# A streaming encoder layer on one core: loads, w_out's first quarters, gate rows and the last scaling in another order

## The chip, the cores and the metric

The kernel runs on one core of a Trainium2 chip. Its time is the device time of one execution in microseconds (us); lower is better. The core has a matrix engine (TensorE, PE in the profile; the loading of its weights is shown apart as PEld), VectorE (DVE), ScalarE (ACT), GpSimd (POOL) and SyncE (SP). Each engine works through its own instructions in order. Transfers (DMAs) are issued from the queues of SP, ACT and POOL and run on 16 DMA engines.

## The reference

One layer of an encoder, for a prompt of 2048 frames and a sample of 32 frames, all in float32, with a width of 1024:

```python
def layer(h, p, ...):
    hn = rmsnorm(h, g_mix)
    proj = hn @ w_in                       # 1024 -> 3072
    hA, bA, cA, zA, vB, zB = jnp.split(proj, ...)
    yA = bA * causal_conv3(cA * hA) * silu(zA)
    yB = (pooled_means(vB) - vB) @ pool_w * pool_scale * silu(zB)
    h = h + concat([yA, yB]) @ w_out       # 1024 -> 1024
    gate = sigmoid(rmsnorm(h, g_ple) @ w_ple_gate)
    h = h + (p @ w_ple) * gate
    return h, new_conv, new_pool
```

A last `rmsnorm(h, g_final)` gives the outputs; the states of the convolution and of the pooling are outputs too.

## The kernel before

**Precision.** Every float32 operand of a product is split into a rounded part (hi) and a remainder (lo): ScalarE casts hi, VectorE computes lo = source - hi (`split`, L79 to L83). A product is the sum of hi x hi, hi x lo and lo x hi, three matmuls for each 128 rows of the inner dimension.

**Stages.** First the input projection w_in, by blocks of 416 frames; then w_out over pairs of tiles of 128 frames (the products o0, o2, ... o14, and a short last one); then the gate with the final scaling (g0 to g14). The stages of w_out and of the gate use a scheme with seven products for a pair of tiles in place of eight (`seven`, L218): of four quarters of the weights (11, 12, 21, 22) and of four parts of the frames it builds sums (S1 to S4 of the frames, T1 to T4 of the weights). Each product takes twelve matmuls; results collect in the banks x_o, y_o and z_o, and VectorE (`carry`, `out`, L1335 to L1352) takes them out. A product that needs a bank afresh waits for that.

**Who sets the order.** A scheduler orders the instructions of each engine from the program text, its estimates and the dependencies; calls of `keep_in_program_order` fix some of them, and `issue_after` holds back a load until an instruction named there has been issued. A reader of a new tile in a pool waits until the pool's previous tile there is free.

**The beginning** (L627 to L789). The frames of the first block are loaded in four tiles (xt; the fourth, of 64 rows, with two loads). ScalarE squares each tile with a sum (L93), POOL forms 1/root (`rstd_of`, L69 to L77), VectorE scales the frames by root and by g_mix, which lies in two PSUM banks, a half each (`first_normal`, L639), PE transposes, ScalarE casts the hi parts (`first_hi`, L661), VectorE the lo parts (L665). Then come three first products zb, v and c (`first_products`, L619). Their weights are loaded by `raw_weight` (L524) where each is needed in the text: zb at L689, v and c at L707. g_mix is copied from PSUM to SBUF as g_bc by two ScalarE copies (L722). Small rows (conv_w, conv_b, pool_scale, the two caches, g_ple) are loaded at L768 to L775 and turned on PE (pv). The second block's frames xt(1,0..2) are loaded in `second_block` (L726).

**w_out's first pair** (L1403 to L1449). w_out's rows come in as wo_q, two halves of columns each; `layout` (L1403) casts quarters 11, 21 and 22 from them. wo_c holds 21's hi, one wo_d its lo, two others 22's hi and lo. In o0 they are cast as soon as `more` (the parts 12, S4 and 22 of the frames) has been issued: 21 and 22 take turns, row by row. PE needs 21 first, in the product y_o.

**The gate's rows** (`scale_gate`, L1379). w_gate's rows are scaled by g_ple once: in each of eight rounds (k) POOL issues two loads (gs, 256 KB each, ring of two), ScalarE scales them (L1391) and stores them to g_d from its own queue (L1392). A new round's loads wait for the stores of the round before. `next_gate` scales the waiting round and issues the next, at the end of each pair and once within o2. After o0, `done_h` (L1361) squares the two finished tiles on ScalarE; POOL's `rs_h` is the root.

**The end** (`last_pair`, L1563; `normed`, L1609). The last pair's second tile is scaled by its root in two parts: 640 columns on VectorE, stored from SP's queue (L1613, L1614), 384 on ScalarE, stored from ScalarE's.

Of the kernel before, what the change touches and what calls it, by code (L numbers as in the profile page):

```python
# [15 lines left out]
P = 128  # L16
# [18 lines left out]
def trunk(ctx, tc, x_p, x_s, c_conv, c_pool, p_p, p_s, g_mix, w_in, conv_w, conv_b, pool_w,  # L35
# [32 lines left out]

    def rstd_of(ssq, n, name, r=None):  # L69

        ms = sm.tile([P, 1], F32, tag="ms", name=f"ms_{name}")
        nc.gpsimd.tensor_scalar(ms[:n], ssq[:n], scalar1=1.0 / D, scalar2=EPS,  # L72
                                op0=ALU.mult, op1=ALU.add)
        if r is None:
            r = sm.tile([P, 1], F32, tag="rstd", name=f"rstd_{name}")
        nc.gpsimd.tensor_tensor(r[:n], ms[:n], nhalf[:n], op=ALU.pow)  # L76
        return r  # L77
# [110 lines left out]
    def frame_parts(cmb, tmp, name, a11, a12, a21, a22):  # L188

        A = {}

        def put(q, src):
            A[q] = cmb.tile([P, KH, 2, P], F32R, tag="c", name=f"{name}_{q}")
            return split(A[q][:, :, 0], A[q][:, :, 1], src)

        def comb(q, x, y, op):
            t = tmp.tile([P, KH, P], F32, tag="s", name=f"{name}_f{q}")  # L200
            nc.vector.tensor_tensor(t, x, y, op=op)
            return t

        s1 = comb("S1", a21, a22, ALU.add)
        put("11", a11)
        s2 = comb("S2", s1, a11, ALU.subtract)
        put("S2", s2)
        put("S1", s1)
        put("S3", comb("S3", a11, a21, ALU.subtract))

        def more():
            put("12", a12)
            put("S4", comb("S4", a12, s2, ALU.subtract))
            return put("22", a22)

        return A, more
# [125 lines left out]
    with ExitStack() as s1:  # L342
# [61 lines left out]

        def x_load(name, rows):

            t, at = ring4(xin, f"xt_{name}"), 0
            for src in rows:
                m = src.shape[0]
                nc.sync.dma_start(t[at:at + m], src)  # L410
                at += m
            return t, at, f"x{name}"
# [6 lines left out]
        def x_tile(name, rows):  # L419
            return x_stat(x_load(name, rows))  # L420
# [103 lines left out]
        def raw_weight(kind, j, name, ring=raw_ring):  # L524
            t = ring(f"raw_{name}")
            col = cols[kind] * WA + j * P
            raw_loads.append(nc.sync.dma_start(t, w_in[:, col:col + P].rearrange("(k p) n -> p k n", p=P)))
            return t
# [99 lines left out]
        ahead0 = [x_load(f"0_{c}", [x_rows(0, c)]) for c in range(3)]  # L628
        short0 = x_load("0_3", [x_rows(0, 3), x_rows(1, 3)])
        B0.update(six(0))  # L630
# [42 lines left out]

        for c in range(3):
            first_x.append(x_stat(ahead0[c], True))
# [13 lines left out]
        raw = raw_weight("zb", 0, "firstzb")  # L689
# [16 lines left out]
        def other_first(kind):  # L706
            raw = raw_weight(kind, 0, f"first{kind}")  # L707
# [11 lines left out]

        first_w.extend(other_first(kind) for kind in ("v", "c"))  # L720
# [5 lines left out]
        def second_block():  # L726
# [3 lines left out]
            for c in range(3):  # L730
                x = x_tile(f"1_{c}", [x_rows(1, c)])
                normal(x)
                xs.append((x, slice(0, P)))
                yield
# [32 lines left out]

        rows = ftile("rows").rearrange("p k n -> p (k n)")[:112, :P]  # L768
        nc.gpsimd.memset(rows, 0.0)
        nc.sync.dma_start(rows[0:12], conv_w[0].rearrange("r (j c) -> (r j) c", c=P))  # L770
        nc.sync.dma_start(rows[12:16], conv_b[0].rearrange("(j c) -> j c", c=P))
        nc.sync.dma_start(rows[16:20], pool_scale[0].rearrange("(j c) -> j c", c=P))
        nc.sync.dma_start(rows[32:40], c_conv[0, 0].rearrange("r (j c) -> (r j) c", c=P))
        nc.sync.dma_start(rows[40:100], c_pool[0, 0].rearrange("r (j c) -> (r j) c", c=P))
        nc.sync.dma_start(rows[100:108].rearrange("k (q c) -> k q c", q=4), g_ple[0].rearrange("(q k c) -> k q c", q=4, k=KC))  # L775
# [540 lines left out]
    with ExitStack() as s2:  # L1316
        pool = lambda name, bufs: s2.enter_context(tc.tile_pool(name=name, bufs=bufs, reuse_waits="tile"))
        w3, qa, xh, st, ss, cmb = (pool(*a) for a in (
            ("w3", 1), ("qa", 2), ("xh", 3), ("st", 4), ("ss", 3), ("cmb", 8)))

        def quarters(name, W):
            c = halves(slot(f"{name}_c"))
            d = {h: w3.tile([P, KH, NH], F32R, tag=f"d{h}", name=f"{name}_d{h}") for h in (1, 0, 2)}
            W.update({"11": c[:2], "21": (c[2], d[0]), "22": (d[1], d[2])})
# [54 lines left out]
        def scale_gate(k):  # L1379
# [6 lines left out]
            for half, t in enumerate(ts):  # L1386
                nc.gpsimd.dma_start(t, rows[:, :, half * NH:half * NH + NH])
# [26 lines left out]
        def rest():  # L1414

            with tc.issue_after(more().ins):
                layout(["21", "22"])
# [12 lines left out]
        for i in range(0, NT - 1, 2):  # L1430
            with tc.issue_after(loaded[-1].ins):
                x = [load_rows(xh, "x", i + b, x_p) for b in range(2)] if i else [first_x, second_x]
            seven(f"o{i}", S.pop(i), W, *h_ops(x, P, f"o{i}", i == 0), {0: {1: rest}, 2: {3: next_gate}}.get(i, {}), True, i == 0)
# [6 lines left out]
            if i + 2 < NT - 1:  # L1440
# [3 lines left out]
                more()  # L1444
# [118 lines left out]
        def last_pair(i, A, before):  # L1563
# [45 lines left out]
            def normed(b, rf):  # L1609
# [3 lines left out]
                fixed(nc.vector.tensor_scalar(o[:, :cut], o[:, :cut], scalar1=rf, scalar2=None, op0=ALU.mult))  # L1613
                nc.sync.dma_start(y[:, :cut], o[:, :cut])  # L1614
# [159 lines left out]
```

## Time and profile before

| | us |
|---|---|
| median of three runs | 921.37 (920.61 to 921.42) |
| the profiled execution | 921.02 |
| span of the profiled execution | 919.2 |
| busy: PE / DVE / ACT / POOL | 905.7 / 722.4 / 481.2 / 159.8 |

The span runs from the first to the last instruction recorded; 1.82 us of the profiled execution lie around it. A line of the timeline reads: start, duration (both us), engine, line of the program, operation, output <- inputs, shape, how many instructions, and in brackets the idle time before and what ended it. "SPq", "ACTq" and "POOLq" are the instructions that issue DMAs. A line of the chain of waits reads: start, duration, what the end of the run was waiting for then. The rows of DMA issues end with the size of one transfer and the median time from issue to landing.

### The profile page before, as it was taken

The page shows a single profiled execution, that of the slowest core. Times are in us where ns is not written, and L with a number is a line of the kernel's source. Part 1 is how long each engine was busy: PE and PEld are TensorE (multiplying, and loading weights), DVE is VectorE, ACT ScalarE, POOL GpSimd, SP SyncE. Part 2 cuts the span into 40 slices and gives each one's busy share as a digit, 9 for nine tenths or more (in the row PEclk, how much of TensorE's full clock was granted, in tenths as well). Part 3 has the DMA queues.
Part 4 walks back from the last instruction along what each step waited for, and adds up shares of the span by engine and source line. Part 5 has one row for each costly group of instructions (what it writes and reads, how often), then busy time and mean ns, then how long its engine had stood idle before and what let it go on. Part 6 is the DMA issues. An engine that isn't in the chain of part 4 may idle for free.

```text
span 919.2 us, 13202 instructions
## 1 busy us (share of the span) xinstructions
PE 905.7 (99%) x4529; PEld 822.7 (90%) x4529; DVE 722.4 (79%) x1236; ACT 481.2 (52%) x894; POOL 159.8 (17%) x307
## 2 busy tenths in 40 slices
PE   8999999999999999999999999999999999999996
PEld 6999999999999999999999987888878878888885
DVE  6996989999576989795777679665558658889885
ACT  7744565654445555443545356334336755555554
POOL 3111222121000333210000120111203301111113
PEclk9999999999999999999999999999999999999998
DMA  9357687798945898638975469865777984676564
GB/s 262 93 145 217 168 249 230 234 294 287 413 131 168 251 227 225 216 122 296 274 228 173 155 243 291 267 189 177 237 228 231 354 263 143 203 242 235 188 209 169
DMA packets 138447, 205.12 MB, mean 223 GB/s; under 512 B 13116, under 2 KB 101724, under 8 KB 137101
## 3 DMA queue, kind: packets, MB, share of 16 engines
q1 hardware_dynamic: 117773, 139.41, 48.9%
q0 software_dynamic: 17872, 59.45, 19.8%
q10 hardware_dynamic: 2736, 5.44, 1.8%
q8 instruction: 35, 0.57, 0.3%
q14 instruction: 31, 0.25, 0.1%
HBM read 136.60 MB, written 67.64 MB: 222 GB/s over the span
## 4 chain that ended last, share of the span: by engine, by line
PE 91%; DVE 3%; DMA 2%; ACT 2%; issue 1%; POOL 0%; SPq 0%; POOLq 0%; DVEq 0%; ACTq 0%
PE x_g L175 9%; PE x_o L175 9%; PE x_zab L591 7%; PE x_zbv L591 6%; PE x_ch L591 5%; PE z_g L175 5%; PE e L107 4%; PE z_o L175 4%; PE z_zab L591 3%; PE h L591 3%; PE z_zbv L591 3%; PE z_ch L591 3%; PE b L591 3%; PE za L591 3%; PE zb L591 2%; PE c L591 2%
## 5 line engine op out<-in xcount | busy, mean ns | idle before, releaser
L80 ACT CAST y_S<-y_fS 128x512 fp32r<-128x512 f32 x32 | 19.5, 622 | 42.2 <-PE x_o L175 20.4
L175 PE MATMUL x_g<-wg_b,g_S 128*128 128x512 f32 x128 | 35.7, 389 | 0.0
L175 PE MATMUL x_o<-wo_b,y_S 128*128 128x512 f32 x128 | 35.6, 390 | 0.0
L591 PE MATMUL x_zab<-B,w_zab_S 128*128 128x416 f32 x168 | 34.2, 352 | 0.2 <-ACT V L987 0.2
L591 PE MATMUL z_zab<-B,w_zab_S 128*128 128x416 f32 x168 | 34.3, 351 | 0.0
L591 PE MATMUL x_zbv<-B,w_zbv_S 128*128 128x416 f32 x168 | 34.2, 352 | 0.0
L591 PE MATMUL z_ch<-B,w_ch_S 128*128 128x416 f32 x168 | 34.1, 351 | 0.0
L591 PE MATMUL z_zbv<-B,w_zbv_S 128*128 128x416 f32 x168 | 34.0, 351 | 0.0
L591 PE MATMUL x_ch<-B,w_ch_S 128*128 128x416 f32 x168 | 34.0, 351 | 0.0
L107 PE MATMUL e<-wq,pps 128*128 128x512 f32 x144 | 33.1, 390 | 0.0
L591 PEld LDWEIGHTS x_zab<-B,w_zab_S 128*128 128x128 f32 x168 | 31.3, 188 | 0.9 <-ACT V L987 0.5
L107 PEld LDWEIGHTS e<-wq,pps 128*128 128x128 f32 x144 | 27.0, 188 | 5.6
L591 PEld LDWEIGHTS z_zbv<-B,w_zbv_S 128*128 128x128 f32 x168 | 31.4, 188 | 0.3
L591 PEld LDWEIGHTS x_ch<-B,w_ch_S 128*128 128x128 f32 x168 | 31.4, 188 | 0.3
L591 PEld LDWEIGHTS z_ch<-B,w_ch_S 128*128 128x128 f32 x168 | 31.3, 188 | 0.3
L591 PEld LDWEIGHTS z_zab<-B,w_zab_S 128*128 128x128 f32 x168 | 31.3, 188 | 0.3
L591 PEld LDWEIGHTS x_zbv<-B,w_zbv_S 128*128 128x128 f32 x168 | 31.3, 188 | 0.4
L1542 DVE SCALAR_TENSOR_TENSOR h<-h,rstd_f,g_bc 128x1024 f32<-128x1024 f32 (+1 forms) x15 | 19.3, 1284 | 14.0 <-POOL rstd_f L76 14.0
L80 ACT CAST y<-y 128x512 fp32r<-128x512 f32 x24 | 14.8, 618 | 29.4 <-PE z_o L175 12.8
L1335 DVE TENSOR_TENSOR c_o<-x_o,x 128x512 f32<-128x512 f32 x14 | 9.7, 691 | 25.7 <-PE x_o L175 25.7
L72 POOL TENSOR_SCALAR ms_f<-ssq_f 128x1 f32<-128x1 f32 (+1 forms) x15 | 6.6, 441 | 128.8 <-ACT junk L93 128.5
L175 PEld LDWEIGHTS x_o<-wo_b,y_S 128*128 128x128 f32 x128 | 23.9, 188 | 5.2 <-ACT c_o L1340 0.3
(591 smaller groups left out, 2694.9 us busy)
## 6 DMA issues: line engine op xcount, KB each, us to landing
y<-y_d SPq DMA_DIRECT2D x16, 512.0 KB, 6.0
x<-in_x_prompt_dram SPq DMA_DIRECT2D x16, 512.0 KB, 6.0
h_d<-x SPq DMA_DIRECT2D x16, 512.0 KB, 4.3
h<-h_d SPq DMA_DIRECT2D x16, 512.0 KB, 3.5
xt<-in_x_prompt_dram SPq DMA_DIRECT2D x15, 512.0 KB, 7.8
e<-e_d SPq DMA_DIRECT2D x15, 512.0 KB, 5.2
out_dram<-h POOLq DMA_DIRECT2D x14, 512.0 KB, 3.0
p_dT<-T POOLq DMA_DIRECT2D x12, 512.0 KB, 6.0
```

The costliest lines, as they stand in the source:

```text
L72: nc.gpsimd.tensor_scalar(ms[:n], ssq[:n], scalar1=1.0 / D, scalar2=EPS, op0=ALU.mult, op1=ALU.add)
L80: ins = nc.scalar.copy(hi, src)
L107: nc.tensor.matmul(ps, pps[:, a, k], wp[k][b][:, cs], start=k + q == 0, stop=k == 1 and q == 2)
L175: nc.tensor.matmul(ps[:n], lhs[:, k, a, :n], w[b][:, k], start=start and k + q == 0, stop=k == KH - 1 and q == 2, skip_group_check=True)
L591: nc.tensor.matmul(ps[:, :NB], lhs[:, k, x], b[:, k, y], start=start and k + q == 0, stop=stop and k == KH - 1 and q == 2, skip_group_chec ...
L1335: add = lambda o, a, b: nc.vector.tensor_tensor(o, a, b, op=ALU.add)
L1542: nc.vector.scalar_tensor_tensor(h[:n], h[:n], rf[:n], g_bc[:n], op0=ALU.mult, op1=ALU.mult)
```

## The change

1. *Small rows and weights at the start.* The six loads of small rows, without g_ple's, move up to just behind the frames. The weights of zb, v and c are loaded together behind them, and zb's load waits for the landing of the third frame tile. The first tile of the second block is issued behind c's load, then g_ple's rows, then the two other tiles.
2. *w_out's first quarters.* `more` is in three parts. 21 is cast after the part 12 has been issued (step 1 of `seven`), 22 after S4 (step 4), and the part 22 of the frames comes last. One of the lo tiles of 22 moves to a pool of its own (w2).
3. *The gate's rows.* Each root is remembered (`roots`), and scale_gate's loads are issued behind the last one. In POOL's queue the first round's loads so stand behind the two roots of o0's tiles; before, they stood ahead of them.
4. *The last scaling.* The second tile's 640 columns are scaled by VectorE and stored by SP in two pieces of 320.

The changed kernel's line numbers are some 20 higher around the gate (L1391 is L1410 there).

```diff
@@ first lines
+    roots = []
...
-        nc.gpsimd.tensor_tensor(r[:n], ms[:n], nhalf[:n], op=ALU.pow)
+        roots.append(nc.gpsimd.tensor_tensor(r[:n], ms[:n], nhalf[:n], op=ALU.pow))
...
-        def more():
-            put("12", a12)
-            put("S4", comb("S4", a12, s2, ALU.subtract))
+        def more(i):
+            if i == 0:
+                return put("12", a12)
+            if i == 1:
+                return put("S4", comb("S4", a12, s2, ALU.subtract))
             return put("22", a22)
...
-        def raw_weight(kind, j, name, ring=raw_ring):
+        def raw_weight(kind, j, name, ring=raw_ring, behind=None):
...
+            if behind is not None:
+                tc.add_manual_dep(raw_loads[-1].ins, behind.ins.name, mybir.DependencyInfo(
+                    mybir.DependencyClass.Sync, mybir.DependencyReason.DATA), reason="leaves the bandwidth to frames")
...
         ahead0 = [x_load(f"0_{c}", [x_rows(0, c)]) for c in range(3)]
+        third_landed = frame_loads[-1]
         short0 = x_load("0_3", [x_rows(0, 3), x_rows(1, 3)])
+
+        rows = ftile("rows").rearrange("p k n -> p (k n)")[:112, :P]
+        nc.gpsimd.memset(rows, 0.0)
+        nc.sync.dma_start(rows[0:12], conv_w[0].rearrange("r (j c) -> (r j) c", c=P))
...
+        nc.sync.dma_start(rows[40:100], c_pool[0, 0].rearrange("r (j c) -> (r j) c", c=P))
...
+        first_raws = {kind: raw_weight(kind, 0, f"first{kind}", behind=third_landed if kind == "zb" else None)
+                      for kind in ("zb", "v", "c")}
+        with tc.issue_after(raw_loads[-1].ins):
+            ahead1 = [x_load("1_0", [x_rows(1, 0)])]
+        nc.sync.dma_start(rows[100:108].rearrange("k (q c) -> k q c", q=4), g_ple[0].rearrange("(q k c) -> k q c", q=4, k=KC))
...
-        raw = raw_weight("zb", 0, "firstzb")
+        raw = first_raws["zb"]
...
-            raw = raw_weight(kind, 0, f"first{kind}")
+            raw = first_raws[kind]
...
+        ahead1 += [x_load(f"1_{c}", [x_rows(1, c)]) for c in range(1, 3)]
         first_w.extend(other_first(kind) for kind in ("v", "c"))
...
-                x = x_tile(f"1_{c}", [x_rows(1, c)])
+                x = x_stat(ahead1[c])
...
-        w3, qa, xh, st, ss, cmb = (pool(*a) for a in (
-            ("w3", 1), ("qa", 2), ("xh", 3), ("st", 4), ("ss", 3), ("cmb", 8)))
+        w3, qa, w2, xh, st, ss, cmb = (pool(*a) for a in (
+            ("w3", 1), ("qa", 2), ("w2", 1), ("xh", 3), ("st", 4), ("ss", 3), ("cmb", 8)))
...
-            d = {h: w3.tile([P, KH, NH], F32R, tag=f"d{h}", name=f"{name}_d{h}") for h in (1, 0, 2)}
+            d = {h: (w2 if h == 2 else w3).tile([P, KH, NH], F32R, tag=f"d{h}", name=f"{name}_d{h}") for h in (1, 0, 2)}
...
-            for half, t in enumerate(ts):
-                nc.gpsimd.dma_start(t, rows[:, :, half * NH:half * NH + NH])
+
+            with tc.issue_after(roots[-1].ins):
+                for half, t in enumerate(ts):
+                    nc.gpsimd.dma_start(t, rows[:, :, half * NH:half * NH + NH])
...
-        def rest():
-
-            with tc.issue_after(more().ins):
-                layout(["21", "22"])
+
+        def lower_left():
+            with tc.issue_after(more(0).ins):
+                layout(["21"])
+
+        def lower_right():
+            with tc.issue_after(more(1).ins):
+                layout(["22"])
+            more(2)
...
-            seven(f"o{i}", S.pop(i), W, *h_ops(x, P, f"o{i}", i == 0), {0: {1: rest}, 2: {3: next_gate}}.get(i, {}), True, i == 0)
+            seven(f"o{i}", S.pop(i), W, *h_ops(x, P, f"o{i}", i == 0), {0: {1: lower_left, 4: lower_right}, 2: {3: next_gate}}.get(i, {}), True, i == 0)
...
-                more()
+                for part in range(3):
+                    more(part)
...
-                fixed(nc.vector.tensor_scalar(o[:, :cut], o[:, :cut], scalar1=rf, scalar2=None, op0=ALU.mult))
-                nc.sync.dma_start(y[:, :cut], o[:, :cut])
+                for cs in (slice(0, cut // 2), slice(cut // 2, cut)) if b else (slice(0, cut),):
+                    fixed(nc.vector.tensor_scalar(o[:, cs], o[:, cs], scalar1=rf, scalar2=None, op0=ALU.mult))
+                    nc.sync.dma_start(y[:, cs], o[:, cs])
```

The scheduler answers with further moves. At the start, ScalarE's order is: the hi parts of the third tile, the two g_bc copies, the two zb casts, the fourth tile's hi parts, then the casts of v and c; before, the two copies came after v's and c's casts. In o2 (the pair that follows o0), the first round's scalings stand on ScalarE ahead of the cast of S1 of the pair o4; before, they stood ahead of it too, with two casts of y between and after them.

## The prediction: does the time move?

> **What bounds the kernel now.** The page first: its span and its busy shares.
>
> ```profile
> span 919.2 us, 13202 instructions
> PE 905.7 (99%) x4529; PEld 822.7 (90%) x4529; DVE 722.4 (79%) x1236; ACT 481.2 (52%) x894; POOL 159.8 (17%) x307
> ```
>
> TensorE is busy for 905.7 of 919.2 us. No matmul is added or removed, so only the remaining 13.5 us, or a new hole in PE, can change the time. The diff touches three such places: the start, the first pair of h tiles (o0), the end. The start comes next, with the chain of waits and the timeline of each engine:
>
> ```profile
> 1.99 6.16 DMA xt<-in_x_prompt_dram
> ...
> 12.01 1.40 DVE xt L639 x2
> 13.40 0.60 DVE B L661
> 14.01 0.61 DVE B L665
> 14.75 1.37 PE zb L619 x6
> ```
>
> ```profile
> 1.13 2.30 SPq L410 DMA_DIRECT2D xt<-in_x_prompt_dram  x5
> 3.48 0.46 SPq L527 DMA_DIRECT2D raw_firstzb<-in_w_in_dram  x1
> 7.10 2.80 DVE L639 SCALAR_TENSOR_TENSOR xt<-xt,rstd_x,gm 128x512 f32<-128x512 f32 x4 [4.92 <-POOL rstd_x L76]
> 10.50 2.90 DVE L639 SCALAR_TENSOR_TENSOR xt<-xt,rstd_x,gm 128x512 f32<-128x512 f32 x4
> 12.88 1.15 ACT L692 CAST w_firstzb<-raw_firstzb 128x512 fp32r<-128x512 f32 x2
> 13.96 0.43 ACT L661 CAST B<-pt 128x128 fp32r<-128x128 f32 x2
> 16.36 1.08 ACT L722 COPY g_bc<-gm 128x512 f32<-128x512 f32 x2
> ```
>
> The chain names the DMA of the third frame until 8.15. VectorE, though, has no gap from 7.10 to 14.62 except about 0.1 us before 12.01 (four steps from 7.10 to 9.90, one remainder, four from 10.50 to 13.40, a cast, a remainder). It starts at 7.10 on the first frame's root. The first product, at 14.75, ends that run, not the wait for the third frame.
>
> In the middle, ScalarE and TensorE in o0:
>
> ```profile
> 554.20 0.62 ACT L1408 CAST wo_c<-wo_q 128x512 fp32r<-128x512 f32 x1
> 554.72 0.62 ACT L1408 CAST wo_d<-wo_q 128x512 fp32r<-128x512 f32 x1
> ```
>
> ```profile
> 553.46 3.01 PE L175 MATMUL x_o<-wo_b,y_S 128*128 128x512 f32 x12
> ...
> 557.99 1.42 PE L170 MATMUL y_o<-wo_c,y 128*128 128x512 f32 x5 [0.53 <-ACT wo_c L1408]
> ...
> 560.18 2.89 PE L170 MATMUL z_o<-wo_d,y_S 128*128 128x512 f32 x12
> 562.90 2.88 PE L175 MATMUL x_o<-wo_T,y 128*128 128x512 f32 x12
> ```
>
> A product of twelve matmuls takes 2.72 us from start to start (560.18 to 562.90). From 553.46 two of them should bring z_o at 558.90; it comes at 560.18. The casts of w_out's quarters hold PE for 1.28 us.
>
> **The change part by part.**
>
> *Frames and rows.* All five frame loads were issued (by 3.43) before the zb weights' load (3.48), so moving the weights later can at most give the frames bandwidth. Even a third frame landing a microsecond earlier moves only the 0.1 us gap: gain 0 to 0.1, and I take 0. [...]
>
> *ScalarE's order at the start.* In the changed program's order the two g_bc copies stand ahead of the zb casts and of the casts of the fourth frame's block (L661, 128x128), of which the first product needs one. The second copy waits there for the last L639, which reads the same bank and ends at 13.40. From there: copy 0.54 (two take 1.08), two zb casts at 0.54 (12.88 to 13.96), one block cast 0.22 (two take 0.43), issue 0.13 (14.62, the end of 14.01's, to 14.75): 13.40 + 0.02 + 0.54 + 1.08 + 0.22 + 0.13 = 15.39, against 14.75: **+0.64**. The zb load, now issued behind the third frame's landing (8.15), has 5.7 us until its cast at 13.9; 512 KB of w_out took 5.5 (row below). Bounds: -0.1 (the copies hidden, the gap gained) to +1.0 (one more cast step from the later products, whose casts are behind the same two copies, or zb some tenths late). I take **+0.6**; afterwards PE has next to no idle that could absorb it.
>
> *w_out in another order.* ScalarE now does the four wo_c casts (quarter 21) right after y_12, where it stands idle before 552.30, and the wo_d casts of 22 later. The timeline, and the loads' issues:
>
> ```profile
> 552.30 0.62 ACT L80 CAST y_S<-y_fS 128x512 fp32r<-128x512 f32 x1 [3.02 <-PE x_o L175]
> ```
>
> ```profile
> wo_q<-in_w_out_dram SPq DMA_DIRECT2D x4, 512.0 KB, 5.5
> ```
>
> The hole of 3.02 us takes four casts of 0.52 (554.20 to 554.72; 2.1 us); their loads took 5.5 us. Hence the 1.28 us goes: **-1.3** (bounds -1.3 to -0.5, where 22's casts and remainders, now the last in that queue, hold z_o).
>
> *Gate's rows.* The rows of w_gate (L1387, two of 256 KB) are scaled by ScalarE and stored. Their loads stood on POOL ahead of the roots of tiles 0 and 1; now they follow them.
>
> ```profile
> 548.08 1.43 POOL L1387 DMA_DIRECT2D gs<-in_w_ple_gate_dram  x2 [0.91 <-DMA e_d<-eout]
> 568.45 0.55 POOL L76 TENSOR_TENSOR rs_h<-ms_h,nhalf 128x1 f32<-128x1 f32 x1
> 574.91 0.75 POOL L1387 DMA_DIRECT2D gs<-in_w_ple_gate_dram  x1 [5.91 <-ACT y_S L80]
> 579.45 0.69 POOL L1387 DMA_DIRECT2D gs<-in_w_ple_gate_dram  x1 [3.79 <-DMA g_d<-gs]
> ```
>
> ```profile
> 570.20 0.33 ACTq L1392 DMA_DIRECT2D g_d<-gs  x1
> 583.29 1.04 ACT L93 ACTIVATE junk<-x 128x1024 bf16<-128x1024 f32 x1
> 584.79 0.73 ACT L1391 ACTIVATE gs<-gs,vec 128x512 f32<-128x512 f32 x1 [0.36 <-DMA gs<-in_w_ple_gate_dram]
> ```
>
> The loads of stretches of the trace, with their median from issue to landing; the first row is 545 to 575, the second 575 to 600:
>
> ```profile
> gs<-in_w_ple_gate_dram POOLq DMA_DIRECT2D x3, 256.0 KB, 11.1
> gs<-in_w_ple_gate_dram POOLq DMA_DIRECT2D x4, 256.0 KB, 6.7
> ```
>
> With o0 shorter by 1.28 the second root ends at 567.7; the two loads issue at 567.75 and 568.5, not at 548.08 and 548.8. ScalarE waits for them in its queue: behind gs_1 stand y_S of S1 and S3 of the next pair; VectorE has their remainders and two sums before `x<-x_o,c_o`, which empties the bank that PE's x_o of T4 needs:
>
> ```profile
> 573.78 2.88 PE L175 MATMUL x_o<-wo_b,y_S 128*128 128x512 f32 x12
> 576.99 0.69 DVE L1335 TENSOR_TENSOR x<-x_o,c_o 128x512 f32<-128x512 f32 x1
> 581.94 2.88 PE L175 MATMUL x_o<-wo_T,y 128*128 128x512 f32 x12
> 591.66 0.69 DVE L1335 TENSOR_TENSOR c_o<-x_o,x 128x512 f32<-128x512 f32 x1 [2.19 <-PE x_o L175]
> ```
>
> If loads land after 8.5 us (between 11.1 and 6.7, by their place in time), gs_1 starts at 577.0; + 0.65 gs_1, 0.6 cast, four VectorE steps at 0.6 (0.69 in the sum's row, overlapped by 0.1) and the sum itself end at 581.3. PE wants it at 581.94 - 1.28 = 580.66: **0.65 us** of stall. Below 7.8 us there is none; at 11.1 it is 3.3.
>
> The stores of the scaled rows follow at 576.9 and 577.7; the second pair of loads stands behind them, 4.7 us after (570.20's store to 574.91): 581.6 and 582.35, instead of 574.91 and 579.45. The load of 579.45 landed after 5.3 (584.79). With that price they land at 586.9 and 587.7. ScalarE then does twice a scaling (0.65) and a square (1.15 with its read), then two casts (0.55): until 591.6; VectorE's second remainder ends at 592.2, c_o at 592.85. PE's x_o with wo_b comes 7 x 2.72 after 573.78, at 592.82, now 592.82 - 1.28 + 0.65 = 592.2: **0.65 us** more, none if both pairs land 0.65 sooner in sum, 2.4 at 7. By the third k it recovers, since one round of store and load needs 4.7 + 6.7 us of the pair's 7 x 2.72. Together **+1.3**, bounds 0 and +5.
>
> [...]
>
> *Last scaling in pieces.*
>
> ```profile
> 914.39 0.55 DVE L1613 TENSOR_SCALAR hg<-hg,rstd_l 128x640 f32<-128x640 f32 x1 [0.83 <-POOL rstd_l L1606]
> 915.03 0.38 ACTq L1616 DMA_DIRECT2D out_dram<-hg  x1
> ```
>
> A piece of 320 columns takes some 0.35, so the first store leaves at 914.8, the second at about 915.1 to 915.4. ScalarE's own store is issued until 915.41 either way, and the bytes are the same: -0.25 to +0.15, taken as **0**.
>
> Sum: +0.6 - 1.3 + 1.3 + 0 = +0.6. The profiled execution took 921.02 (its span and 1.82 around it), 0.35 below the median of 921.37; +0.6 on the median gives **922.0 us**.
>
> **The rivals.**
>
> 1. *Rows come in time.* POOL's loads share nothing with SP's backlog, or 512 KB less in the stretch before 578 lets the first pair land within 7 us and the second within 5.3. For: the median of 6.7 after 575. Against: the 11.1 of the pair issued in o0. The sum is +0.6 - 1.3 = -0.7, **920.7**. If the start costs nothing too (-1.3): **920.1**, and with a gain at start and end (-0.1 - 0.25) 919.7. [...]
> 2. *Rows come late* (slower). ScalarE, queued behind its gate scalings, keeps PE waiting 2.1 us where the first loads need 10 us, and 2.4 more where the second need 7. It decides from about 9.5 us of the first. +0.6 - 1.3 + 2.1 + 2.4 = +3.8: **925.2**. For: the row of 11.1, and the new issue lies in its stretch; against: that stretch ends at 575, while these loads run.
> 3. *w_out's order doesn't help*, because 22's remainders or the y load hold PE at z_o instead (0.5 of 1.28 gained): 922.0 + 0.8 = **922.8**.
>
> **How the numbers follow.** Forecast 0.40, rows in time 0.25 (a third of it with no loss at the start), rows late 0.23, w_out's order without help 0.12. About 0.2% (1.84 us) is what a measurement of this kernel can tell from no change: 919.5 to 923.2. Faster then holds only in part of rival 1: 0.12. Slower is rival 2 (0.23) and the upper parts of forecast and rival 3, which lie 1.2 and 0.4 below the bound: 0.17; in all 0.40. Same: 0.48. The range of 8 in 10 reaches from rival 1's lower form to between forecast and rival 2's point: **919.8 to 924.8**.
>
> **What would show it.** First product at 15.3 to 15.5 behind ScalarE's block cast (a start at 14.7 refutes the +0.6). No wait of y_o for wo_c; z_o 5.4 us behind x_o's wo_b. POOL's gate loads right behind the second root, ScalarE idle for DMA gs before L1410, and PE idle twice, before x_o of T4 and x_o with wo_b of the next pair, 0.65 each. The prediction is wrong if gs is never waited for, if PE gets idle at any other place, or if the end moves by over 0.3.

## The result: slower, and the profile after

| | before | after |
|---|---|---|
| median | 921.45 us (920.61 to 923.69, 6 runs) | 928.93 us (927.40 to 929.90, 6 runs) |
| ratio to before | | 1.0075 [1.0065, 1.0086] |
| profiled execution / its span | 921.02 / 919.2 us | 928.77 / 926.9 us |

The ratio and its interval are worked out from all the runs, so they need not be the quotient of the two medians. The time lies above the whole range (919.8 to 924.8). First the page of the changed kernel, its span and busy shares, then its waits of PE ("waited for": us in total, times, the longest).

```profile
span 926.9 us, 13209 instructions
PE 908.4 (98%) x4529; PEld 824.4 (89%) x4529; DVE 720.8 (78%) x1237; ACT 480.3 (52%) x894; POOL 160.0 (17%) x307
```

```profile
PE x_o L177 <- ACT y L82: 3.6, 1, 3.6
...
PE zb L628 <- ACT B L679: 1.4, 1, 1.4
```

PE's busy time grew by 2.7 us with the same 4529 matmuls, and its holes by 5. So there are two kinds of loss: waits, and matmuls that ran longer. The second kind shows in the granted clock of the start (0.67 of full speed in 16 to 20 us, 1.00 before). Each row of this view is a stretch, and PEclk stands behind the busy times of the five engines; first the changed kernel, then the kernel before:

```profile
16.00:20.00 4.00, 3.85 (x14) 3.75 (x15) 4.00 (x10) 3.87 (x9) 0.49 (x1) 0.67 1.02 393
20.00:24.00 4.00, 4.00 (x22) 3.90 (x21) 3.01 (x6) 2.77 (x6) 3.58 (x6) 0.90 1.02 283
```

```profile
16.00:20.00 4.00, 4.00 (x23) 3.93 (x22) 3.88 (x9) 3.12 (x7) 0.06 (x1) 1.00 0.95 335
```

In 16 to 20 us PE issued 14 matmuls where it issued 23 before. The trace's clock records put it down to one piece: half clock from 17.39 for 3.41 us. The timeline of the start, changed kernel:

```profile
9.21 0.40 SPq L533 DMA_DIRECT2D raw_firstzb<-in_w_in_dram  x1
9.28 1.06 ACT L95 ACTIVATE junk<-xt 128x1024 bf16<-128x1024 f32 x1 [1.87 <-DMA xt<-in_x_prompt_dram]
13.75 1.15 ACT L748 COPY g_bc<-gm 128x512 f32<-128x512 f32 x2
14.79 1.14 ACT L717 CAST w_firstzb<-raw_firstzb 128x512 fp32r<-128x512 f32 x2
15.83 0.44 ACT L679 CAST B<-pt 128x128 fp32r<-128x128 f32 x2
16.15 2.12 PE L628 MATMUL zb<-B,w_firstzb 128*128 128x416 f32 x8 [1.36 <-ACT B L679]
```

The order on ScalarE is the predicted one (copies, zb casts, block cast, first product). But the third frame was squared at 9.28, and the first product came at 16.15, 1.40 later than before. PE had idled for 1.36 us ahead of it, where it idled for 0.83 before:

```profile
14.75 1.75 PE L619 MATMUL zb<-B,w_firstzb 128*128 128x416 f32 x8 [0.83 <-DVE B L665]
```

In the middle, POOL's loads, ScalarE and PE of the changed kernel:

```profile
571.81 0.90 POOL L78 TENSOR_TENSOR rs_h<-ms_h,nhalf 128x1 f32<-128x1 f32 x1
572.67 1.51 POOL L1406 DMA_DIRECT2D gs<-in_w_ple_gate_dram  x2
582.33 0.72 ACT L1410 ACTIVATE gs<-gs,vec 128x512 f32<-128x512 f32 x1 [9.18 <-DMA gs<-in_w_ple_gate_dram]
584.22 0.72 ACT L1410 ACTIVATE gs<-gs,vec 128x512 f32<-128x512 f32 x1 [1.18 <-DMA gs<-in_w_ple_gate_dram]
589.24 3.01 PE L177 MATMUL x_o<-wo_T,y 128*128 128x512 f32 x12 [3.64 <-ACT y L82]
591.85 0.72 ACT L1410 ACTIVATE gs<-gs,vec 128x512 f32<-128x512 f32 x1 [2.73 <-DMA gs<-in_w_ple_gate_dram]
```

The two loads landed 9.7 and 10.8 us after their issue (572.67 to 582.33; 573.4, the middle of the two, to 584.22). ScalarE stood 9.18 and 1.18 us for them, PE 3.64. And w_out's first pair:

```profile
557.95 2.88 PE L177 MATMUL x_o<-wo_b,y_S 128*128 128x512 f32 x12
560.67 1.98 PE L172 MATMUL y_o<-wo_c,y 128*128 128x512 f32 x8
562.48 1.07 PE L172 MATMUL y_o<-wo_d,y 128*128 128x512 f32 x4
563.39 2.88 PE L172 MATMUL z_o<-wo_d,y_S 128*128 128x512 f32 x12
```

z_o follows wo_b's product by 5.44 us, where it took 6.72: the 1.28 were won (1.14 where every matmul is matched with its own start before).

**Where the time went**, by matching each matmul with the same one before and taking the difference of their starts; the places are times of the kernel before: +2.97 us at 43 us, +3.84 at 152, +4.56 at 471, +4.35 at 556, +3.21 at 560 (w_out's gain), +3.50 at 580, +7.40 at 583 (the gate's rows), +7.63 at 601, +7.9 at the last, and +7.7 for the span.

### The profile page after: what moved, and what is told of

It reads as the page before. It is cut to its first block, busy times and chain, and to the rows that moved or that the text cites. A ratio compares the mean times of both kernels' runs of the same rounds, so it can differ in the third digit from the quotient of the medians.

```text
span 926.9 us, 13209 instructions
## 1 busy us (share of the span) xinstructions
PE 908.4 (98%) x4529; PEld 824.4 (89%) x4529; DVE 720.8 (78%) x1237; ACT 480.3 (52%) x894; POOL 160.0 (17%) x307
## 3 DMA queue, kind: packets, MB, share of 16 engines
q10 hardware_dynamic: 2736, 5.44, 1.8%
## 4 chain that ended last, share of the span: by engine, by line
PE 86%; DMA 5%; DVE 5%; ACT 3%; issue 1%; POOL 0%; SPq 0%; POOLq 0%; DVEq 0%; ACTq 0%
PE x_g L177 9%; PE x_o L177 8%; PE x_zab L600 7%; PE x_zbv L600 6%; PE x_ch L600 5%; PE z_g L177 5%; PE e L109 4%; PE z_o L177 4%; PE z_zab L600 3%; PE z_zbv L600 3%; PE z_ch L600 3%; PE za L600 3%; PE b L600 3%; PE h L600 2%; PE y_g L177 2%; PE zb L600 2%
## 5 line engine op out<-in xcount | busy, mean ns | idle before, releaser
L177 PEld LDWEIGHTS x_g<-wg_b,g_S 128*128 128x128 f32 x128 | 24.0, 188 | 5.0
```

Of the source, the lines that this page charges most:

```text
L177: nc.tensor.matmul(ps[:n], lhs[:, k, a, :n], w[b][:, k], start=start and k + q == 0, stop=k == KH - 1 and q == 2, skip_group_check=True)
```

## The experiments

Each kernel is the kernel before or the changed one with parts exchanged. The kernel before ran beside them each time: median 922.1 for the first four, 921.6 for the next three, 922.0 for the last five.

| | kernel | median us | ratio to before, 95% |
|---|---|---|---|
| e1 | before + gate's part | 927.27 | 1.0059 [1.0042, 1.0076] |
| e2 | same, loads behind the first root | 931.79 | 1.0102 [1.0081, 1.0124] |
| e3 | before + w_out's part + the end | 924.07 | 1.0022 [1.0010, 1.0035] |
| e4 | before + the beginning | 924.96 | 1.0029 [1.0015, 1.0043] |
| e5 | e4, copies behind the casts | 925.12 | 1.0029 [1.0015, 1.0043] |
| e6 | e4, filler work on PE | 924.90 | 1.0033 [1.0023, 1.0043] |
| e7 | e3, frames' part 22 earlier | 922.33 | 1.0006 [0.9994, 1.0018] |
| e8 | before, 21 cast ahead of 22 | 920.78 | 0.9994 [0.9982, 1.0006] |
| e9 | e1, rows scaled later | 926.71 | 1.0045 [1.0031, 1.0059] |
| e10 | after without the gate's part | 925.17 | 1.0038 [1.0026, 1.0051] |
| e11 | e8 + the end | 920.81 | 0.9980 [0.9970, 0.9990] |
| e12 | before + small rows early | 924.79 | 1.0027 [1.0016, 1.0038] |

### The gate's part: e1, e2, e9

e1 takes that part of the change alone:

```diff
+        roots.append(nc.gpsimd.tensor_tensor(r[:n], ms[:n], nhalf[:n], op=ALU.pow))
...
+            with tc.issue_after(roots[-1].ins):
+                for half, t in enumerate(ts):
+                    nc.gpsimd.dma_start(t, rows[:, :, half * NH:half * NH + NH])
```

> The kernel before with the gate's rows issued behind the last root and nothing else of the change. Theory (ScalarE stands for the late rows): loads issued near 569, landing after 9 to 11 us, ScalarE idle for them by some 9 us in o2, PE idle by about 4 us before x_o of T4; 925.4 us. Rival 1 (the wait is as the prediction sized it, 8.5 and 5.3 us to landing): +1.3, 922.7. Rival 2 (the wait of the whole change came from the shifted start meeting other transfers): no wait here, 921.4.

ScalarE waited 7.29 us and 1.44 for the rows, and PE then stood at another product than in the changed kernel:

```profile
571.50 1.51 POOL L1391 DMA_DIRECT2D gs<-in_w_ple_gate_dram  x2
579.85 0.72 ACT L1395 ACTIVATE gs<-gs,vec 128x512 f32<-128x512 f32 x1 [7.29 <-DMA gs<-in_w_ple_gate_dram]
584.71 4.58 PE L177 MATMUL z_o<-wo_d,y_S 128*128 128x512 f32 x12 [2.83 <-DVE c_o L1337]
```

The product behind the hole took 4.58 us, where twelve take 2.9: a piece of half clock (granted 0.66 in 585 to 590 us and 1.00 in the 5 us ahead, so 3.4 us of it) follows the stall and adds 1.7. So the gate's part costs some 5 us on its own, and late rows are its first cause. That is the theory's mechanism. Its hole was too long (about 4 us, measured 2.83), and its total, without the half clock, is 1.9 too low.

e2 issues the same loads behind the root of the first tile:

```diff
-            with tc.issue_after(roots[-1].ins):
+            with tc.issue_after(roots[-2].ins):
```

> As e1, but the loads stand behind the first of the two roots, some 2.2 us earlier in POOL's queue. Theory (each us of the issue is a us of the wait): the loads land about 2 us earlier and PE's wait shrinks from 4 to about 2 us; 923.4. Rival (the landing is set by the end of the crowded stretch on the DMA engines, not by the issue): as e1, 925.4.

```profile
567.26 1.50 POOL L1391 DMA_DIRECT2D gs<-in_w_ple_gate_dram  x2
580.85 0.72 ACT L1395 ACTIVATE gs<-gs,vec 128x512 f32<-128x512 f32 x1 [10.72 <-DMA gs<-in_w_ple_gate_dram]
584.76 4.98 PE L177 MATMUL x_o<-wo_b,y_S 128*128 128x512 f32 x12 [10.23 <-ACT y_S L82]
```

```profile
570.00:575.00 5.00, 4.53 (x20) 3.40 (x19) 1.62 (x3) 0.13 (x1) 0.00 (x0) 1.00 1.02 202
575.00:580.00 5.00, 0.00 (x0) 0.00 (x0) 0.00 (x0) 0.00 (x0) 0.00 (x0) 0.88 1.00 170
580.00:585.00 5.00, 0.24 (x1) 0.28 (x2) 2.89 (x5) 3.36 (x6) 0.75 (x1) 0.50 0.45 154
585.00:590.00 5.00, 5.00 (x14) 3.94 (x15) 3.44 (x7) 0.38 (x2) 0.69 (x1) 0.60 0.69 172
```

The last two numbers of a row are the DMA share and GB/s. The loads left 4.2 us earlier than in e1 and landed no earlier (580.85 against 579.85), after 13.6 us. Until 580 the DMA engines are occupied without a gap (share 1.0) at no more than 170 to 202 GB/s; when the share falls to 0.45 the rows are there. So the earlier issue gained nothing here, as the rival said. That the end of such a stretch sets the landing is not shown: e9, below, has loads that landed in the middle of one. The times of theory and rival both fail. ScalarE asks for the rows ahead of o4's y casts here, so VectorE and PE stand too (10.23 us), and half clock runs for some 10.2 us from 578.8 (0.88, 0.50 and 0.60 in the three rows from 575), the last 4.2 of them behind the hole.

e9 keeps e1's late loads, but takes the extra scaling step out of o2 and puts it into o6:

```diff
-            seven(f"o{i}", S.pop(i), W, *h_ops(x, P, f"o{i}", i == 0), {0: {1: rest}, 2: {3: next_gate}}.get(i, {}), True, i == 0)
+            seven(f"o{i}", S.pop(i), W, *h_ops(x, P, f"o{i}", i == 0), {0: {1: rest}, 6: {3: next_gate}}.get(i, {}), True, i == 0)
```

> The kernel before with the gate's loads behind the roots (as e1), and the extra scaling step moved from the middle of o2 to the middle of o6: the first round's rows are scaled at the end of o2, some 10 us later than in e1, ahead of o4's y casts. The loads are as late as in e1 (landing near 580 and 582), but ScalarE asks for them after 583. Theory: e1's loss is ScalarE standing in its queue for them; with nothing asked before they land, PE has no hole in o2 and o4 and the time is that of before, 921.6 (within 1). Rival: the loads' place in the crowded stretch itself costs (they take bandwidth from y and x loads, which come later): PE still has a wait for DMA or for VectorE's c_o in o2, and 1.5 us or more remain (923 and above).

In o2 and o4 nothing is lost: the difference to the kernel before is +0.6 us at 471 and stays between 0.0 and 0.1 from 556 to 617. The first round's loads were not as late as in e1:

```profile
569.04 1.50 POOL L1391 DMA_DIRECT2D gs<-in_w_ple_gate_dram  x2
```

They landed at 576.1 and 578.1, 7.0 and 8.3 us after their issue, while the DMA engines' share was 0.79 (570 to 575) and 0.97 (575 to 580); in e1, with 0.97 and 1.05 there, the same loads took 8.3 and 9.7. Then e1's loss comes in o6:

```profile
606.82 0.74 POOL L1391 DMA_DIRECT2D gs<-in_w_ple_gate_dram  x1
616.56 0.73 ACT L1395 ACTIVATE gs<-gs,vec 128x512 f32<-128x512 f32 x1 [9.27 <-DMA gs<-in_w_ple_gate_dram]
619.77 4.58 PE L177 MATMUL z_o<-wo_d,y_S 128*128 128x512 f32 x12 [2.27 <-DVE c_o L1337]
```

The loads behind the roots as such take nothing from the others in o2; the price is ScalarE asking for rows that have not landed while its later casts are wanted. In o2 (e1) and in o6 (here) the extra step follows its round's loads by half a pair, and loads of 8 to 10 us did not fit. The first theory's total fails, since it left out that the step needs a place; the rival's total fits, but it looked for the loss in o2, where there is none.

### w_out's order and the end: e3, e7, e8, e11

e3 takes the change of w_out's quarters and the end in pieces, on the kernel before:

```diff
...
-        def rest():
-            with tc.issue_after(more().ins):
-                layout(["21", "22"])
+        def lower_left():
+            with tc.issue_after(more(0).ins):
+                layout(["21"])
+        def lower_right():
+            with tc.issue_after(more(1).ins):
+                layout(["22"])
+            more(2)
...
```

> The kernel before with w_out's new order and the last scaling in two pieces, without the new start and the gate's rows. Theory: the 1.28 us of wait in o0 go and stay gone, the end gains 0.2; 921.4 - 1.5 = 919.9. Rival (the gain is given back, by the y load or by ScalarE's later queue in o2): 921.2 to 921.6.

```profile
557.41 4.01 SPq L328 DMA_DIRECT2D y<-y_d  x2
```

```profile
567.60 0.69 DVE L201 TENSOR_TENSOR y_fS<-y,y 128x512 f32<-128x512 f32 x1 [2.18 <-DMA y<-y_d]
570.88 0.50 PE L175 MATMUL x_o<-wo_a,y_S 128*128 128x512 f32 x1 [2.06 <-DVE c_o L1337]
```

The gain in o0 is there (1.13: from -0.58 at 556 to -1.71 at 560), and 10 us later it is more than spent (+1.18 at 570): VectorE waits 2.18 us for frames of o4, ahead of the c_o that empties PE's bank. Their buffer is held by o0's frames until part 22 of them is cast, and the change puts that cast last, behind w_out's: the load leaves at 557.41, in the kernel before at 555.05:

```profile
555.05 0.38 SPq L326 DMA_DIRECT2D y<-y_d  x1
```

Half clock follows (a matmul of x_o takes 0.63 us at 572.83, where it took 0.39 at 571.91), and at 580 the program is 2.23 behind.

e7 casts that part ahead of quarter 22:

```diff
         def lower_right():
-            with tc.issue_after(more(1).ins):
-                layout(["22"])
-            more(2)
+            s4 = more(1)
+            more(2)
+            with tc.issue_after(s4.ins):
+                layout(["22"])
```

> e3 with the frames' part 22 cast ahead of w_out's quarter 22 instead of behind it. Theory (y's buffer was held by that cast, so the next pair's second y load was issued at 557.4 instead of 555.0 and VectorE stood 2.2 us for it in o2): load issued by 555.5, no wait for y on VectorE, PE keeps the 1.3 us; 1.3 to 1.5 below the kernel before. Rival (VectorE's wait comes from the shorter o0 itself: the load is no later, it is only asked for sooner): the wait of about 2 us stays, time at or above before.

The load leaves at 556.33, VectorE's wait falls to 1.49 us and PE's to 1.38, with no half clock (single matmuls of x_o behind it take 0.39 or 0.40 us), and the median is 1.2 us nearer to that of before than e3's (+0.7 in place of +2.0). The theory's mechanism holds, but only about half of the delay is undone, and its time (1.3 to 1.5 below the kernel before) did not come.

e8 leaves the frames' parts as they were and changes only the order of the casts:

```diff
             with tc.issue_after(more().ins):
-                layout(["21", "22"])
+                layout(["21"])
+                layout(["22"])
```

> The kernel before with one change: the parts 12, S4 and 22 of o0's frames are issued together as before, and behind them ScalarE casts all four rows of quarter 21 and only then those of 22, in place of row by row in turn. Theory: in e3 the second frame load of o4 came later because part 22's cast had moved behind w_out's casts; here y_22 is cast at 553.7 as before, 21's four casts (0.52 each) end at about 556.3, ahead of the 556.71 at which PE wants y_o. So z_o follows x_o's wo_b by 5.44 us (before 6.72), the second load of o4 leaves ScalarE's queue point unchanged (555.1), and VectorE does not wait for y. Time: the 1.28 us of the hole is kept, 920.3 where before's median is 921.6 (ratio 0.9986). Rival: PE gone ahead by 1.28 us makes the y load late by itself, whatever the cast's place, since o4's loads run behind a queue that does not get faster: VectorE waits for y by about 1.3 us more, PE stands at o2's x_o again, and the time is that of before (921.6) or above it by a window of half clock (1.7).

The trace shows no wait of PE for wo_c and none of VectorE for y. z_o comes 5.57 us after wo_b's product, and of the 1.14 won there (from +2.28 at 556, a jump at 443 us included, to +1.14 at 560) 1.0 is left at 580 (+1.28). The theory's reading of the trace holds, but this interval includes no change. With the end in pieces added, e11 tells it:

```diff
-                fixed(nc.vector.tensor_scalar(o[:, :cut], o[:, :cut], scalar1=rf, scalar2=None, op0=ALU.mult))
-                nc.sync.dma_start(y[:, :cut], o[:, :cut])
+                for cs in (slice(0, cut // 2), slice(cut // 2, cut)) if b else (slice(0, cut),):
+                    fixed(nc.vector.tensor_scalar(o[:, cs], o[:, cs], scalar1=rf, scalar2=None, op0=ALU.mult))
+                    nc.sync.dma_start(y[:, cs], o[:, cs])
```

> e8's order of quarters (21's four casts ahead of 22's, the frames' parts as before) and the last scaling in two pieces, on the kernel before. Theory: both gains are real and independent: 0.8 of the hole in o0 and 0.2 at the end, 1.0 in all: 920.9 where before's median is 921.9 (ratio 0.9989), and the profile shows z_o 5.5 us after x_o's wo_b, no wait for y in o2. Rival: e8's median was chance (its interval held 1), jumps elsewhere in the program outweigh it and the ratio is 0.9997 or above.

```profile
554.18 2.18 ACT L1408 CAST wo_c<-wo_q 128x512 fp32r<-128x512 f32 x4
556.27 2.18 ACT L1408 CAST wo_d<-wo_q 128x512 fp32r<-128x512 f32 x4
...
569.84 0.50 PE L175 MATMUL x_o<-wo_a,y_S 128*128 128x512 f32 x1 [0.35 <-DVE c_o L1335]
```

0.9980 [0.9970, 0.9990] is faster than the kernel before, clear of noise: for the gain in o0, 21's four casts in one go suffice, and the frames keep their buffer's time. Of 1.14 won in o0, 0.4 is left at 580 in this execution, behind a wait of 0.35 and another order of x_o's and z_o's products; the end is 0.2 shorter. So the median's 1.2 is larger than what the trace adds up to (0.6 here, 1.2 with e8's 1.0).

### The beginning: e4, e5, e6, e12

e4 has the beginning of the changed kernel alone:

```diff
+        nc.sync.dma_start(rows[0:12], conv_w[0].rearrange("r (j c) -> (r j) c", c=P))
...
+        first_raws = {kind: raw_weight(kind, 0, f"first{kind}", behind=third_landed if kind == "zb" else None)
+                      for kind in ("zb", "v", "c")}
+        with tc.issue_after(raw_loads[-1].ins):
+            ahead1 = [x_load("1_0", [x_rows(1, 0)])]
...
+        ahead1 += [x_load(f"1_{c}", [x_rows(1, c)]) for c in range(1, 3)]
```

> The kernel before with the new start alone. Theory (the third frame lands a us later, ScalarE's two copies follow, PE's clock is halved for one window, and two later waits of 0.9 near 150 and 0.7 near 470 come from it too): first product 1.4 later, 3.0 by 43 us, 4.5 by 475; 925.9. Rival 1 (the two later waits belong to other parts): 924.4. Rival 2 (the prediction's +0.6): 922.0, clock full.

```profile
2.00 6.02 DMA xt<-in_x_prompt_dram
```

```profile
14.97 2.47 PE L624 MATMUL zb<-B,w_firstzb 128*128 128x416 f32 x8 [1.36 <-ACT B L675]
```

Here the third frame landed at 8.02 (8.15 before, 9.19 in the changed kernel's profile). The first product comes 0.22 later than before, the eight matmuls take 2.47 in place of 1.75, and at 24 us the program is 1.8 behind: half clock from 15.8 (0.97 in 12 to 16 us, 0.60 in 16 to 20, 1.00 in 20 to 24) costs 1.6. The median is 2.9 above that of before, nearest to rival 1; this execution, at 922.57, was one of the fastest.

e5 fixes the casts of v and c, as those of zb already were, ahead of the two copies in ScalarE's order (the difference to e4):

```diff
-                nc.scalar.copy(t[:, :, 0], raw[:, half * KH:half * KH + KH])
+                in_turn(nc.scalar.copy(t[:, :, 0], raw[:, half * KH:half * KH + KH]))
...
-            nc.scalar.copy(g_bc[:, half * NH:half * NH + NH], pg[half])
+            in_turn(nc.scalar.copy(g_bc[:, half * NH:half * NH + NH], pg[half]))
```

> e4's new start, with the two g_bc copies held behind the casts of v and c as in the kernel before. Theory (the copies alone make the first product late and leave PE idle long enough for its clock to be halved): the first product stands 6.4 to 6.6 us behind the third frame's landing instead of 6.95, PE's idle time before it is some 0.8 instead of 1.36, the clock stays full, time within 0.7 of the kernel before. Rival (loads of weights or rows hold the start): 6.95, halved clock, 924 to 925.

The first product's idle is 0.83 again and the clock full there (its eight matmuls take 1.73 us, 1.75 before). But c's weights are late then (0.63 us of wait on ScalarE), the copies end near 18.8, and the second block's first product pays:

```profile
35.31 0.46 PE L596 MATMUL zb<-B,w_firstzb 128*128 128x416 f32 x1 [1.59 <-ACT B L80]
```

Half clock follows: the fourteen matmuls of zb from 35.97 take 4.37 us, in the kernel before twenty-three from 33.57 take 4.50. In this execution the loss moved to the next queue position, and the median stayed (925.12, where the theory had at most 0.7 above before's 921.6).

e6 fills PE's idle time with six transposes that nobody reads. It also fixes the place of the small rows' turning (pv) in PE's order, which changed nothing that the trace shows: it comes at 20.6, in e4 at 20.8. The difference to e4:

```diff
+            for _ in range(6):
+                in_turn(nc.tensor.transpose(out["zb"][:, :P], ident, ident))
...
```

> e4's new start with six more transposes of the identity on PE, which go to the bank of the first product while PE waits for it; nothing reads them. Theory (the halved clock costs 1.2 to 1.5 us, and it comes from PE's idle time): clock full from 0 to 25 us, first product still 6.95 behind the landing, PE at 40 us some 1.2 earlier than in e4 at the same landing; about +0.5 on the kernel before. Rival (the clock is halved at the start of some executions whatever PE does): half a clock window again, as e4.

```profile
15.07 0.85 PE L612 MATMUL zb<-ident 128*128 128x128 f32 x6 [0.61 <-DVE B L683]
16.01 1.76 PE L626 MATMUL zb<-B,w_firstzb 128*128 128x416 f32 x8
```

The clock stayed full (1.00 in all three stretches from 12 to 24), and at 24 us the program was 1.2 behind before, in e4 1.8. But the first product came 7.56 us after the third frame's landing, where e4 had 6.95, and the median did not move. That the clock costs time here is shown by the two traces; that it makes most of e4's median is not.

e12 moves the small rows' loads alone (five of them; g_ple's stays), and leaves the weights' where they were in the text:

```diff
         short0 = x_load("0_3", [x_rows(0, 3), x_rows(1, 3)])
+        rows = ftile("rows").rearrange("p k n -> p (k n)")[:112, :P]
+        nc.gpsimd.memset(rows, 0.0)
+        nc.sync.dma_start(rows[0:12], conv_w[0].rearrange("r (j c) -> (r j) c", c=P))
...
```

> The kernel before with the six loads of small rows alone moved up behind the frames; the weights' loads stay where they were in the text, and no load waits for a landing. The scheduler's answer on ScalarE is the same as in the changed kernel (both g_bc copies ahead of the zb casts). Theory: the start's loss is that order on ScalarE with the half clock behind it, not the place of the weights' loads: first product 6.9 to 7.0 us after the third frame's landing (before 6.6), PE's idle at the first product 1.2 to 1.4, a window of half clock behind it, and 924.5 to 925.3 with before at 921.9, like e4. Rival: the weights' wait for the third frame makes the loss: the zb casts here have their data early, the first product comes 6.4 to 6.6 after the landing, and the time is 921.5 to 922.5.

```profile
4.92 0.27 SPq L636 DMA_DIRECT2D rows<-in_cache_conv_dram  x1
6.18 0.32 SPq L637 DMA_DIRECT2D rows<-in_cache_pool_dram  x1
9.13 0.40 SPq L527 DMA_DIRECT2D raw_firstzb<-in_w_in_dram  x1
```

```profile
16.07 2.29 PE L619 MATMUL zb<-B,w_firstzb 128*128 128x416 f32 x8 [1.36 <-ACT B L669]
```

The first product comes 6.95 us after the third frame's landing (9.12), with 1.36 of idle and half clock from some 17.1 (0.64 in 16 to 20 us, 0.94 in 20 to 24): e4's picture, and its time by the median (this execution, at 927.93, was the slowest of twelve). The zb load goes out at 9.13 although no written wait holds it. In the trace these loads take turns with eight semaphores, so that from the ninth on a load waits for the landing of the one eight places ahead: the caches' rows left at 4.92 and 6.18, as the first two frames landed (4.90, 6.17). With five small loads put between, zb's is eight behind the third frame's. So the change's explicit wait changes nothing once the rows stand there. The run can't tell late weights apart by their issue, but ScalarE's timeline does: it has no gap between 10.26 and the zb casts, so nobody waited for them, and for the first product the order on ScalarE is what is left.

For the median it is not shown. At some 42 us the six profiled kernels with the new start are 0.8 to 4.0 us behind the one before (2.1 in the mean), the other seven from 0.6 ahead to 0.9 behind, so most of the loss arises in the beginning. But e5, with the old order, and e6, with the clock full, have it in their medians as well. All four share the early rows, and weights that leave only when the third frame has landed; what makes the rest of the loss stays open.

### The sum of the parts: e10

The changed kernel without the gate's part:

```diff
-            with tc.issue_after(roots[-1].ins):
-                for half, t in enumerate(ts):
-                    nc.gpsimd.dma_start(t, rows[:, :, half * NH:half * NH + NH])
+            for half, t in enumerate(ts):
+                nc.gpsimd.dma_start(t, rows[:, :, half * NH:half * NH + NH])
```

> The changed kernel with the gate's part undone (beginning, w_out's order and the end as changed). Theory of added parts: e4's +3.4 (924.96 against 921.6) and e3's +2.5 (924.07) stand by themselves, and the two sum to 921.6 + 5.9 = 927.5; the changed kernel's 928.9 then holds only 1.4 of the gate. Theory of one shared hole: w_out's loss is a y load that comes late in o4, at the place where the gate's late rows hold ScalarE anyway in the changed kernel; then this kernel has the start's loss (about 3) and w_out's (2.5) but a start that is late shifts the y loads too, so that part of the 2.5 goes: 925 to 926.5, and the gate's part is worth 2.5 to 4 beside it.

It stands 3.2 us above before, e4 and e3 together 4.8. That is the second theory's number, but its reason isn't in the trace: PE's hole at o2's x_o is there in full.

```profile
573.07 0.50 PE L175 MATMUL x_o<-wo_a,y_S 128*128 128x512 f32 x1 [2.15 <-DVE c_o L1350]
```

This execution had no piece of half clock, neither behind that hole (single matmuls of 0.39 us from 573.41) nor behind 1.56 us of idle at the first product (eight matmuls in 1.76); its mean granted clock was 0.999. The profiles of e3 and e4 (0.996 each) hold one such piece each, which is one difference between the traces. For the medians the difference is not clear of noise: e10's interval reaches from 2.4 to 4.7 us, and the two others have intervals as wide. The gate's part is worth the rest of the changed kernel's loss, 7.5 - 3.2 = 4.3.

## Why the prediction was wrong

Two terms failed: the gate's rows, mis-sized by 2.6 us but inside their bounds (0 to +5), and the start, mis-sized by 2.4 and beyond its bounds (-0.1 to +1.0).

**Gate's rows: the landing was mis-sized.** The chain was right (loads behind the second root, ScalarE standing in its queue, PE idle before T4's x_o). The prediction took 8.5 us to landing, between 11.1 and 6.7; it was 9.7 and 10.8, which is rival 2's case, with its 2.1 us of PE stall measured as 3.64. In the prediction's own steps: the second load's landing adds 2.2 us, and the way from the second scaling to PE's product, 5.0 us (584.22 to 589.24) in place of 4.3, adds 0.7, in part because ScalarE issued the store of the scaled row (0.33) ahead of its cast; 0.65 + 2.2 + 0.7 = 3.6. The profile names the cast of y as what PE waited for; it ended at 589.11, 0.02 after the sum that the prediction had named. The error lies in taking one price between two medians. The 16 such loads in the trace of before took from 5.3 to 11.9 us, and the first round behind the roots took 8.3 and 9.7 in e1, 13.6 and 13.8 in e2, 7.0 and 8.3 in e9. The second stall (0.65, rival 2: 2.4) did not come: the second round's loads took 5.2 and 6.1, near the 5.3 of the prediction, and with PE already late, ScalarE waited 2.73 for them without anyone behind it. Beside before, the gate's part cost 3.9 us in this trace (+3.50 to +7.40) against 1.3 in the sum.

**ScalarE's order at the start: right, but the clock was left out.** From landing to first product the kernels with the old order took 6.60 (before) and 6.43 (e1), those with the new one 6.96 (after), 6.95 (e4, e12): +0.35 to +0.5 for +0.6. (In e10 it took 0.9 more; eight transposes took 1.91 us there from 9.96, in the kernel before 1.04 from 9.72.) What the sum lacked is the clock: PE's idle grew from 0.83 to 1.36, and half clock for 3.4 us behind it cost 1.6 by 24 us in each of the changed kernel, e4 and e12. No step of the prediction looked at the granted clock: that is the step that failed here.

**Frames and rows: the 0 held, its reason only half.** The landing of the third frame varied between executions of either order: ScalarE squared it between 7.88 and 9.36 in eight executions with the old order, 7.99 to 9.28 in six with the new. The changed profile has one of the late ones, 1.0 us of its 2.97. But the prediction let a landing move only a gap of 0.1 us. For a later one that is wrong: in e1, with the start of before, a landing 1.0 later brought the first product 0.85 later. For an earlier one no run tells the third frame apart (in e9 all three frames were squared 0.3 to 0.4 earlier, and the first product came 0.5 earlier).

**w_out in another order: -1.3 held where it was looked for.** What failed is that nothing was late next. Rival 3 had named the y load, but at z_o; it came one pair later. It costs 0.3 in the changed kernel (+3.21 to +3.50) and 3.9 in e3 (-1.71 to +2.23 at 580, half clock included), as the last cast of o0's frames frees the buffer of o4's.

**The last scaling: 0 predicted, -0.2 measured** (last matmul +7.9, span +7.7), within its bounds; e3, e7, e10 and e11, which have this part too, show the same 0.2.

The changed profile's 7.7 us, where the sum had +0.6, are so: start 3.0 (landing 1.0, order 0.4, clock and what follows it 1.6), w_out -1.14 + 0.29, gate 3.9, end -0.2. The remaining 1.9 are small jumps, above all between 43 and 152 (+0.9) and up to 471 us (+0.7). Jumps at those places come and go in kernels whose code there is that of before (e9: from -0.8 at 141 to +0.3 at 152; e8: from -0.9 to +2.9 around 445, where 24 matmuls took 6.08 us from 444.87 and the next 24 4.53), so they are not shown to be the change's.

## What to carry to other kernels

Price a moved load by the loads of equally full stretches, and with their whole spread: here the same 256 KB load took from 7.0 to 13.8 us, and an issue 4.2 us earlier (e2) did not bring the landing forward. Where an engine works in order, ask what stands behind the instruction that waits (ScalarE stood 9.18 us for the gate's rows, PE 3.64 behind it), and when a buffer that it frees is loaded next; e8's order, which moved casts but no buffer's last reader, kept the gain that the change lost again. And a hole in PE may cost more than its length, since in some of these runs the matmuls behind it ran at half clock (1.6 us more for 1.36 of idle at the start).

## What had not been expected of the hardware

- *Half clock behind short holes.* Between the first products and the last, half clock followed holes of PE of 1.36 us (the changed kernel, e4, e12), 1.59 (e5), 2.06 (e3), 2.27 (e9) and 2.83 (e1) and began within that of 10.23 (e2); it did not follow those of 0.83 (before), 1.38 (e7), 1.56 and 2.15 (e10) or 3.64 (the changed kernel, with 1.00 from 588 to 596 us). The piece was 3.41 us long in the changed kernel; the rows of e1, e4 and e12 add up to 3.4, those of e2 to 10.2. In e3, e5 and e9 it shows in the matmuls behind the hole (in e9 twelve took 4.58 us, where they take 2.9). So the length of a hole alone does not tell whether half clock follows: 1.56, 2.15 and 3.64 us went without it, 1.36 in three kernels did not. What decides it wasn't settled.
- *Full DMA engines at half the rate.* In e2 the share was 1.0 at 170 to 202 GB/s, in the changed kernel's start 1.02 at 393. A 256 KB load took 13.6 us in the first. Why the same share moves half as much wasn't settled.
